# Splitting the operands of the second feed-forward half where they are made, and fetching them as two stored parts

## The chip, the core and the metric

The kernel runs on one core of one Trainium2 chip. The core has five engines that run side by side, each working through its own queue in order: TensorE (PE, with its weight loads as PEld), VectorE (DVE), ScalarE (ACT), GpSimd (POOL) and SyncE (SP), which here only issues transfers. Sixteen DMA engines move the data between HBM and the on-chip memory; a transfer can be issued from SP's, ScalarE's or GpSimd's queue. The metric is the device time of one execution in microseconds, lower being better.

## The reference

One inference step of a one-layer encoder on 640 frames (512 of a prompt, 8 x 16 of samples) of width 2048: an input projection, two groups of attention heads, an output projection, and a gated feed-forward layer of width 5632. The change touches only the feed-forward layer:

```python
def merge_and_ffn(x, oa, ob, norm_grp_a, norm_grp_b, w_out, norm_ffn, w_gate, w_up, w_down):
    o = jnp.concatenate([rmsnorm(oa, norm_grp_a), rmsnorm(ob, norm_grp_b)], axis=-1)
    x = x + o @ w_out
    h = rmsnorm(x, norm_ffn)
    return x + (jax.nn.silu(h @ w_gate) * (h @ w_up)) @ w_down
...
    y_prompt = rmsnorm(xp, norm_final)
    y_sample = rmsnorm(xs, norm_final)
```

## The kernel before

Everything is kept transposed, features on the 128 partitions and the 640 frames in two halves of `HT` = 320 columns along the row. All matrix products are of 32-bit values in TensorE's rounded format, and to keep the precision each operand is written as the sum of two rounded parts: `hi`, a rounded copy made by ScalarE, and `lo`, the rest, made by a subtraction on VectorE or GpSimd. `mm3` (lines 186 to 190) then issues three matmuls, hi x hi, hi x lo and lo x hi. Weights are split the same way after they are loaded: `split`, line 179 on ScalarE and line 180 on VectorE.

**Quartets.** The feed-forward products use a scheme with seven block products in place of eight (`quartet`, lines 870 to 922). Four weight blocks are loaded by SP (line 890); VectorE makes two differences of them (903 and 905), GpSimd two more (907 and 914); then come the products in the order p1, p6, p7, p2, p5, p4, p3. Each product splits its weights, multiplies them with `k` pairs of operands and leaves a PSUM bank that VectorE adds to the result tiles (line 924). The split weights lie in three pairs of tiles, so the split of a product waits until the product three before it has been read by TensorE. Of the weight tiles there are six, so loads run about one quartet ahead.

**The first half** (lines 957 to 1008). For each of the 22 pairs `i` of 128-row blocks of the inner width there is a quartet over `w_gate` and one over `w_up`, 44 in all, each of 7 x 8 x 3 matmuls. The left operands are the eight pairs of rows of the normed input, in seven combinations each, all held on the chip as split tiles (56 of the 62 tiles of list "S"). After the gate quartet VectorE, ScalarE and GpSimd apply the norm and the SiLU (990 to 992); after the up quartet VectorE multiplies gate and up (996), GpSimd makes four combinations (1000 to 1003: s1, s3, s2, s4), and the seven operands of the pair for the second half are stored unsplit to `act_d` in HBM, 128 x 320 values each, in four transfers (1005 and 1007), by SP, or by GpSimd for the last pair.

**The second half** (lines 1019 to 1064). The product with `w_down` runs in 32 steps. In a step five or six of the 22 pairs are active (`START`, `active`, lines 31 to 36); a pair stays for eight steps, one for each of eight pairs of output rows, which are kept in 20 tiles of "S". So the seven operands of a pair are fetched just before it becomes active. Pairs 0 to 4 are active at the start and come back at the end, so that 27 x 7 = 189 operands are loaded in all.

- `free` (946 to 955) is called after each product of the last quartet of the first half. It gives up the eight tiles of the combination just used and loads the operands of that combination for pairs 0 to 4, two pairs to a transfer, and splits them: `hi` on ScalarE (line 936), `lo` on VectorE for pairs 0, 2 and 4 and on GpSimd for 1 and 3 (line 941).
- `fetch` (928 to 944) does it for one operand. It loads the 160 KB into a spare "S" tile or one of two scratch tiles `half` (line 934), makes `hi` on ScalarE (936) and `lo` by a subtraction (941) on VectorE (combinations 0, 3 and 6) or GpSimd. In steps 16 to 29 it makes `lo` another way: ScalarE writes minus `hi` (938), and a GpSimd transfer loads the operand again and adds it (939).
- `fetch_waiting` keeps the fetches of a combination back until two more products have been issued.

The order of instructions in each engine's queue is made by a scheduler from the order of the program and the dependencies; a tile is written again only when all that read it, transfers included, are done.

## Time and profile before

| | |
|---|---|
| Median of three runs | 2653.87 us (2651.46 to 2653.96) |
| Profiled execution | 2658.85 us, of which the span from first to last instruction is 2657.1 us |
| PE busy | 2590.4 us, 97% |
| DVE, ACT, POOL busy | 1894.7, 1112.5 and 765.4 us |
| HBM read and written | 284.70 and 54.20 MB |
| Transfers on the hardware queue and on GpSimd's queue | 326.92 and 11.47 MB |
| Granted TensorE clock, mean | 0.992 |

The stages can be told apart by the lines that run in them: the first half of the feed-forward layer fills 1000 to about 2060 us, the 32 steps over `w_down` about 2060 to 2643 us, and the last 14 us scale and store the output.

How to read the rows: an engine's busy time counts its instructions, not its waits. A row of the view of groups gives line, engine, operation, output and inputs, the shape, the count, then busy time and mean nanoseconds of one, then the idle time of the engine just before these instructions and what ended it. In the views of order, the bracket at the end of a row is that idle time. "W" are weight tiles, "S" tiles of activations, "dn" and "at" PSUM banks, "half" the scratch tiles. A wait is put down to the event that came last.

### The profile page before, as it was taken

To read this page: it belongs to the slowest core of one execution; us is meant where nothing else is said; L and a number is where in the kernel's file an instruction comes from. 1 tells how busy PE (TensorE), PEld (TensorE's weight loads), DVE (VectorE), ACT (ScalarE), POOL (GpSimd) and SP (SyncE) were. 2 spreads that over 40 slices of the span, in tenths; PEclk is the share of its full clock that TensorE was granted. 3 is DMA by queue.
4 is the path that set the end of the run, shared out by engine and by line. 5 is a ranking of instruction groups with operands and counts; after the bars stand their busy time and mean duration, and the time that the engine had idled before them with its cause. 6 is when DMAs were issued, how large, how long until landed. Compare 5 with 4: busy or idle time off the path is not lost.

```text
span 2657.1 us, 44937 instructions
## 1 busy us (share of the span) xinstructions
PE 2590.4 (97%) x17565; PEld 2532.0 (95%) x17565; DVE 1894.7 (71%) x2934; ACT 1112.5 (42%) x1830; POOL 765.4 (29%) x584
## 2 busy tenths in 40 slices
PE   8999999999999999999999999999999899999996
PEld 8999998999899999999999999999999899999996
DVE  5665566655866877676676677667667988878797
ACT  5443344444633543333333333333334444455553
POOL 0000000000211223433433433343345533444463
PEclk9999999999999999999999999999999899999998
DMA  5322232433655433333333333333335744467665
GB/s 169 106 72 80 90 103 87 129 119 128 221 179 182 155 118 101 118 105 103 123 99 112 119 105 105 114 105 108 119 103 167 222 135 126 134 152 179 154 154 154
DMA packets 162549, 342.58 MB, mean 129 GB/s; under 512 B 19072, under 2 KB 77440, under 8 KB 162336
## 3 DMA queue, kind: packets, MB, share of 16 engines
q1 hardware_dynamic: 151824, 326.92, 38.9%
q0 software_dynamic: 9360, 11.47, 2.7%
q8 instruction: 138, 2.26, 0.4%
q10 hardware_dynamic: 1152, 1.31, 0.1%
q14 instruction: 75, 0.61, 0.1%
HBM read 284.70 MB, written 54.20 MB: 128 GB/s over the span
## 4 chain that ended last, share of the span: by engine, by line
PE 70%; DVE 6%; DMA 3%; issue 2%; ACT 2%; SPq 0%; POOL 0%; DVEq 0%; ACTq 0%; POOLq 0%
PE dn L188 14%; PE dn L190 14%; PE dn L189 14%; PE at L188 9%; PE at L189 9%; PE at L190 9%; DVE W L180 2%; PE at L303 1%; DMA S<-act_d 1%; DVE S L924 1%; DMA W<-w_down 1%; DVE S L180 1%; DMA S<-cka 1%; ACT W L179 1%; DVE S L941 0%
## 5 line engine op out<-in xcount | busy, mean ns | idle before, releaser
L188 PE MATMUL dn<-S,W 128*128 128x320 f32 x3694 | 1161.4, 314 | 11.8 <-DVE S L924 5.5
L190 PE MATMUL dn<-S,W 128*128 128x320 f32 x3694 | 1148.6, 311 | 14.5 <-DVE W L180 14.3
L189 PE MATMUL dn<-S,W 128*128 128x320 f32 x3694 | 1146.6, 310 | 2.0 <-DVE S L180 1.1
L179 ACT ACTIVATE W<-W 128x1024 fp32r<-128x1024 f32 (+2 forms) x632 | 608.2, 963 | 1024.6 <-PE dn L189 538.5
L180 DVE TENSOR_TENSOR W<-W,W 128x1024 fp32r<-128x1024 f32 (+2 forms) x632 | 761.1, 1204 | 157.8 <-ACT W L179 152.6
L188 PEld LDWEIGHTS dn<-S,W 128*128 128x128 f32 x3694 | 697.3, 189 | 24.5 <-issue 9.2
L190 PEld LDWEIGHTS dn<-S,W 128*128 128x128 f32 x3694 | 696.9, 189 | 20.5 <-DVE W L180 19.1
L189 PEld LDWEIGHTS dn<-S,W 128*128 128x128 f32 x3694 | 697.4, 189 | 4.6 <-DVE S L180 1.3
L190 PE MATMUL at<-S,W 128*128 128x320 f32 x1594 | 494.6, 310 | 4.2 <-DVE W L180 4.1
L188 PE MATMUL at<-S,W 128*128 128x320 f32 x1594 | 493.5, 310 | 0.0
L189 PE MATMUL at<-S,W 128*128 128x320 f32 x1594 | 493.3, 309 | 0.0
L907 POOL TENSOR_TENSOR W<-W,W 128x1024 f32<-128x1024 f32 (+2 forms) x76 | 163.4, 2150 | 583.1 <-DVE W L180 502.0
L190 PEld LDWEIGHTS at<-S,W 128*128 128x128 f32 x1594 | 299.8, 188 | 7.7 <-DVE W L180 7.4
L189 PEld LDWEIGHTS at<-S,W 128*128 128x128 f32 x1594 | 300.1, 188 | 0.0
L188 PEld LDWEIGHTS at<-S,W 128*128 128x128 f32 x1594 | 300.0, 188 | 0.0
L924 DVE TENSOR_TENSOR S<-S,dn 128x320 f32<-128x320 f32 x358 | 164.2, 481 | 100.6 <-PE dn L190 99.4
L903 DVE TENSOR_TENSOR W<-W,W 128x1024 f32<-128x1024 f32 (+2 forms) x76 | 135.6, 1784 | 102.9 <-DMA W<-w_up 50.7
L914 POOL TENSOR_TENSOR W<-W,W 128x1024 f32<-128x1024 f32 (+2 forms) x76 | 165.4, 2177 | 105.9 <-DVE W L180 102.8
L924 DVE TENSOR_TENSOR S<-S,at 128x320 f32<-128x320 f32 x262 | 123.3, 480 | 71.2 <-PE at L190 71.2
L262 POOL TENSOR_TENSOR S<-S,S 128x640 f32<-128x640 f32 x40 | 74.6, 1865 | 156.6 <-ACT S L261 153.4
L905 DVE TENSOR_TENSOR W<-W,W 128x1024 f32<-128x1024 f32 (+2 forms) x76 | 82.8, 1090 | 33.4 <-DMA W<-w_gate 25.8
L517 POOL MEMSET S<- 80x640 f32 x9 | 6.3, 695 | 330.0 <-DMA ob_d<-S 212.2
(153 smaller groups left out, 2269.2 us busy)
## 6 DMA issues: line engine op xcount, KB each, us to landing
W<-w_gate SPq DMA_DIRECT2D x88, 512.0 KB
W<-w_up SPq DMA_DIRECT2D x88, 512.0 KB
W<-w_in SPq DMA_DIRECT2D x66, 512.0 KB
W<-w_down SPq DMA_DIRECT2D x64, 384.0 KB
W<-w_down SPq DMA_DIRECT2D x68, 320.0 KB
act_d<-S SPq DMA_DIRECT2D x63, 320.0 KB
half<-act_d SPq DMA_DIRECT2D x81, 160.0 KB
S<-act_d SPq DMA_DIRECT2D x80, 160.0 KB
```

The lines of the kernel that those rows point to most:

```text
L179: self.nc.scalar.activation(hi, src, AF.Identity)
L180: self.nc.vector.tensor_tensor(lo, src, f(hi), ALU.subtract)
L188: mm(out, a[0], b[0], start=first, stop=False)
L189: mm(out, a[0], b[1], start=False, stop=False)
L190: mm(out, a[1], b[0], start=False, stop=last)
L262: (eng or nc.gpsimd).tensor_tensor(ssq, ssq, sq, ALU.add)
L303: nc.tensor.transpose(out, src, n.ident)
L903: nc.vector.tensor_tensor(b12[:, w], b12[:, w], b22[:, w], sub)
L905: nc.vector.tensor_tensor(s6[:, w], b11[:, w], b12[:, w], sub)
L907: nc.gpsimd.tensor_tensor(b11[:, w], b22[:, w], s6[:, w], sub)
L914: nc.gpsimd.tensor_tensor(b21[:, w], b21[:, w], s6[:, w], sub)
L924: add = lambda o, a, b: nc.vector.tensor_tensor(o, a, b, ALU.add)
```

## The change

The split moves from the second half into the first. When a pair is finished, its seven operands are put on a list `parts`; `store_part` takes one from the list at a time: ScalarE makes `hi` into a scratch tile, VectorE makes `lo` (over the operand itself, or for pairs 0 to 3 into another scratch tile), and SP stores both to `act_d`, which now has room for two parts. One part is handled at the end of the pair, one after each further product of the next gate quartet, and for the last pair one after each product of step 0. A result tile goes back to its list when its parts are stored, and the second result tile of each quartet is taken only after p6.

A fetch is then one transfer of 320 KB from GpSimd's queue into the tile, with no arithmetic. Only `free` still splits, for pairs 0 to 3, from unsplit copies that are stored beside (`first_d`); pair 4 is fetched.

```diff
-    def fetch(j, which, raw=None, engine=nc.gpsimd):
...
+    def fetch(j, which):
+        t = n.get("S")
+        hl = pack(t, HT)
+        nc.gpsimd.dma_start(out=r(sh(t, 2, HT)), in_=r(act_d[which, :, j]))
         lefts[j][which] = t, hl
 
     def free(which):
         n.put("S", *(h[which][0] for h in hs))
         ready = active(0)
-        for j in ready[::2]:
-            k = min(2, ready[-1] + 1 - j)
+        for j in ready[:-1:2]:
             raw = n.get("S")
-            dma(out=sh(raw, k, HT), in_=act_d[which, :, j:j + k])
-            for a in range(k):
-                fetch(j + a, which, raw[:, a * HT:a * HT + HT], (nc.vector, nc.gpsimd)[a])
+            dma(out=sh(raw, 2, HT), in_=first_d[which, :, j:j + 2])
+            for a, engine in enumerate((nc.vector, nc.gpsimd)):
+                t = n.get("S")
+                hi, lo = hl = pack(t, HT)
+                part = raw[:, a * HT:a * HT + HT]
+                nc.scalar.activation(hi, part, AF.Identity)
+                engine.tensor_tensor(lo, part, f(hi), ALU.subtract)
+                lefts[j + a][which] = t, hl
             n.put("S", raw)
+        fetch(ready[-1], which)
+
+    parts = []
+
+    def store_part():
+
+        if parts:
+            j, which, src, done = parts.pop(0)
+            if j < len(active(0)) - 1:
+                dma(out=first_d[which, :, j], in_=src)
+            hi = n.scratch()
+            nc.scalar.activation(r(hi), src, AF.Identity)
+            if j < len(active(0)) - 1:
+                lo = n.scratch()
+                nc.vector.tensor_tensor(r(lo), src, hi, ALU.subtract)
+            else:
+                lo = src
+                nc.vector.tensor_tensor(r(lo), src, hi, ALU.subtract)
+            dma(out=act_d[which, :, j, 0], in_=hi)
+            dma(out=act_d[which, :, j, 1], in_=lo)
+            n.put("S", *done)
...
-            y = n.get("S"), n.get("S")
-            c11, c21, c12, c22 = y[0][:, :HT], y[0][:, HT:], y[1][:, :HT], y[1][:, HT:]
+            y = [n.get("S")]
+            c11, c21 = y[0][:, :HT], y[0][:, HT:]
...
                 elif step == "p6":
+                    y.append(n.get("S"))
+                    c12, c22 = y[1][:, :HT], y[1][:, HT:]
                     add(c12, c11, bank)
...
+                if step != "p1":
+                    store_part()
...
-                store = nc.gpsimd.dma_start if i == NPAIR - 1 else dma
-                store(out=act_d[0, :, i], in_=c11)
-                for t, pick in ((w, slice(1, 7, 5)), (u, slice(2, 4)), (y[1], slice(4, 6))):
-                    store(out=act_d[pick, :, i].rearrange("w p c -> p w c"), in_=halves(t))
-                n.put("S", *gate, *y)
+                parts = [(i, 0, c11, [y[0]]), (i, 1, s2, []), (i, 6, s4, [w]), (i, 2, s3, []),
+                         (i, 3, s1, [u]), (i, 4, c12, []), (i, 5, c22, [y[1]])]
+                store_part()
```

24 lines of the change are left out of this document (5 added, 19 removed).

## The prediction

> **What bounds the kernel now.** I read the page's busy shares first, then stretches of 20 to 300 us, then the waits of each engine, and last the order of instructions at a pair boundary. First the page:
>
> ```profile
> span 2657.1 us, 44937 instructions
> ...
> PE 2590.4 (97%) x17565; PEld 2532.0 (95%) x17565; DVE 1894.7 (71%) x2934; ACT 1112.5 (42%) x1830; POOL 765.4 (29%) x584
> ```
>
> TensorE is the bound almost everywhere, so an edit pays only where PE loses time. The view of stretches shows where (columns: length, busy time and count of PE, PEld, DVE, ACT, POOL, granted clock, DMA share, GB/s). The first row is one gate quartet; the others belong to the turn from the first half into w_down and to the w_down stage:
>
> ```profile
> 1513.90:1538.50 24.60, 24.60 (x170) 24.60 (x169) 16.42 (x18) 8.50 (x9) 9.34 (x7) 1.00 0.43 140
> ...
> 2040.00:2060.00 20.00, 16.83 (x111) 15.88 (x109) 20.00 (x23) 15.38 (x34) 12.74 (x11) 1.00 0.79 262
> 2060.00:2080.00 20.00, 15.26 (x69) 14.26 (x70) 19.85 (x23) 7.12 (x15) 16.21 (x16) 0.66 0.72 242
> 2080.00:2100.00 20.00, 18.58 (x123) 17.69 (x122) 18.70 (x28) 9.12 (x17) 7.68 (x7) 1.00 0.75 234
> ...
> 2180.00:2200.00 20.00, 17.89 (x121) 17.39 (x120) 17.26 (x25) 9.74 (x17) 7.68 (x6) 1.00 0.46 133
> 2200.00:2500.00 300.00, 300.00 (x2047) 300.00 (x2046) 242.56 (x326) 146.45 (x235) 126.08 (x97) 1.00 0.60 150
> 2500.00:2600.00 100.00, 93.93 (x617) 90.17 (x616) 85.76 (x128) 56.15 (x102) 55.39 (x45) 1.00 0.65 152
> 2600.00:2620.00 20.00, 14.09 (x78) 12.33 (x77) 19.08 (x27) 9.65 (x19) 10.56 (x8) 0.91 0.46 141
> ```
>
> Undisturbed, a matmul takes 300/2047 = 0.1466 us. At that pitch the rows lose: 20 - 111 x 0.1466 = 3.7 us, then 9.9 and 2.0 (the turn, 15.6 together), 2.3 at 2180, 9.5 in 2500 to 2600, 8.6 in 2600 to 2620. The prize is 36 us; the gate quartet has nothing to win and something to lose. PE's waits after 2060 us, and behind them those of ACT and DVE in 2500 to 2600 and after 2600 (us, times, longest):
>
> ```profile
> PE dn L190 <- DVE W L180: 9.4, 9, 2.4
> PE dn L188 <- DVE S L924: 5.5, 3, 3.1
> PE at L190 <- DVE W L180: 4.1, 8, 1.6
> PE dn L188 <- ACT S L936: 2.9, 2, 2.1
> ```
> ```profile
> ACT S L936 <- DMA S<-act_d: 23.4, 11, 3.5
> ```
> ```profile
> DVE W L180 <- ACT W L179: 6.7, 5, 1.8
> DVE W L903 <- DMA W<-w_down: 5.6, 6, 1.6
> ```
> ```profile
> ACT S L936 <- DMA S<-act_d: 5.4, 5, 2.1
> ```
> ```profile
> DVE W L180 <- ACT W L179: 3.9, 3, 3.5
> ```
>
> PE waits for VectorE. VectorE in turn waits for ScalarE's weight split (L179), which stands in ScalarE's queue behind the operand split L936, and L936 waits for its transfer. That chain is what the change takes out.
>
> **What is removed, and what each costs.** The operand work of the second half, by shape:
>
> ```profile
> L939 POOL DMA_DIRECT2D S<-act_d x63 | 55.3, 886 | 85.1 <-ACT S L938 71.4 <-PE at L190 7.6 <-PE dn L190 2.7
> L936 ACT ACTIVATE S<-S 128x320 fp32r<-128x320 f32 x108 | 47.7, 464 | 56.7 <-DMA S<-act_d 55.8 <-DVE S L941 0.6
> ...
> L941 POOL TENSOR_TENSOR S<-S,S 128x320 fp32r<-128x320 f32 x41 | 45.0, 1105 | 45.8 <-ACT S L936 33.3 <-PE dn L190 6.9 <-PE dn L189 5.3
> ...
> L936 ACT ACTIVATE S<-half 128x320 fp32r<-128x320 f32 x81 | 37.3, 460 | 14.7 <-DMA half<-act_d 12.4 <-POOL S L941 1.3 <-DVE S L941 0.8
> ...
> L941 DVE TENSOR_TENSOR S<-S,S 128x320 fp32r<-128x320 f32 x41 | 35.0, 875 | 1.8 <-ACT S L936 1.8
> ...
> L941 POOL TENSOR_TENSOR S<-half,S 128x320 fp32r<-128x320 f32 x25 | 32.5, 1303 | 51.0 <-ACT S L936 50.9
> ...
> L938 ACT ACTIVATE S<-S 128x320 fp32r<-128x320 f32 x63 | 29.5, 470 | 1.7
> ...
> L941 DVE TENSOR_TENSOR S<-half,S 128x320 fp32r<-128x320 f32 x19 | 10.3, 544 | 0.1
> ```
>
> That is 189 operands: 35 split in `free`, 154 fetched later. After the change 28 are still split in `free` (four pairs, seven operands), 14 subtractions on VectorE and 14 on GpSimd; 161 come by one GpSimd transfer. ScalarE loses 161 x 0.46 + 29.5 = 104 us, VectorE 46 subtractions, GpSimd 52. GpSimd gains 98 transfers (161 for 63) at 0.886: 87 us, against 52 x 1.18 = 61 us and the last pair's four stores gone; it stays about where it is.
>
> The turn. In 2030 to 2060 and 2060 to 2080, L941 alone (DVE, POOL):
>
> ```profile
> 2030.00:2060.00 30.00, 14.31 (x15) 14.33 (x12) 1.00 0.69 222
> 2060.00:2080.00 20.00, 6.83 (x8) 6.14 (x6) 0.66 0.72 242
> ```
>
> VectorE is full from 2040 to 2080. `free` now gives it 14 subtractions instead of 21: 7 x 14.31/15 = 6.7 us less. The last pair's seven parts bring back seven at 0.48 to 0.95, so 3.4 to 6.7 us, later and spread over step 0. Net 3.3 at best of VectorE's. In 2060 to 2080 PE is idle 4.7 of the 9.9 us; the other 5.2 is the clock, granted at 0.66 after a 2.1 us wait for L936. I take 3.3 plus half of 5.2: 6 us; bounds -3 (the parts cost more than `free` saves) and 13.
>
> At 2180 the 2.3 us are waits behind L936 and its subtractions; none is left: 2 us. In 2500 to 2600 VectorE gets back up to the 6.7 us that it waits for L179, while 5.6 for weights stay; PE's steps with no fetch lose too, so I take two thirds, 4.5 of 9.5 us (0 to 8). In 2600 to 2620 likewise the 3.9 us: 4 of 8.6 (0 to 7). Sum of gains: 6 + 2 + 4.5 + 4 = 16.5 us.
>
> **What is added, and what covers it.** Each pair now costs seven ScalarE copies and seven VectorE subtractions, six of them in the next gate quartet: 7 x 0.46 = 3.2 us on 8.50 and 7 x 0.54 to 0.95 = 3.8 to 6.7 us on 16.42, of 24.60. Both fit, VectorE with 1.5 us to spare at worst. Stores go from 4 to 14 on SP's queue (21 for the first four pairs), 1.1 to 2.2 MB or about 46 GB/s more on 140, at a DMA share of 0.43. Where do they stand? At a pair's end today (VectorE, GpSimd, SP, PE):
>
> ```profile
> 1521.31 0.49 DVE L924 TENSOR_TENSOR S<-S,dn 128x320 f32<-128x320 f32 x1 [0.99 <-PE dn L190]
> 1524.46 1.23 DVE L903 TENSOR_TENSOR W<-W,W 128x1024 f32<-128x1024 f32 x1 [2.66 <-DMA W<-w_up]
> 1525.61 1.22 DVE L180 TENSOR_TENSOR W<-W,W 128x1024 fp32r<-128x1024 f32 x1
> ```
> ```profile
> 1517.40 0.88 POOL L1002 TENSOR_TENSOR S<-S,S 128x320 f32<-128x320 f32 x1
> ```
> ```profile
> 1515.48 4.14 SPq L1007 DMA_DIRECT2D act_d<-S  x3
> 1519.71 0.42 SPq L890 DMA_DIRECT2D W<-w_up  x1
> ```
> ```profile
> 1527.98 0.31 PE L188 MATMUL dn<-S,W 128*128 128x320 f32 x1
> 1528.13 0.31 PE L189 MATMUL dn<-S,W 128*128 128x320 f32 x1
> 1528.27 0.31 PE L190 MATMUL dn<-S,W 128*128 128x320 f32 x1
> ```
>
> Today SP sits in the stores, and a weight load behind them goes out only at 1519.71; VectorE waits 2.66 us for it, then does the split that ends at 1526.83 and is read at 1528.27: 1.4 us of slack, the smallest that I found in the first half. With stores spread over the quartet that load can go sooner (below nothing: a small gain, but PE is full, so worth 0); a store that waits for a late subtraction can block it as today. I price the first half at 0.
>
> The new fetch waits in GpSimd's own queue for a free tile, ahead of L907 and L914, for whose results the weight splits of p5 and p4 wait. In the L939 row GpSimd already waits 13 us for PE in 63 such transfers, and 2200 to 2500, which holds most of them, loses nothing. I take 1.5 us (0 to 8).
>
> The landing: GpSimd's issue and, on the same line, the time to landing:
>
> ```profile
> L939 POOL DMA_DIRECT2D S<-act_d x63: 842/857/1187, 2342.7 to 2591.9; - x63
> ...
> DMA to landing us min/median/max: 3.4/4.5/8.2
> ```
>
> A GpSimd load of 320 KB that only copies isn't in this trace; the nearest is this one, of 160 KB with an addition, and I take its median, with 3.4 and 8.2 as ends. A group is fetched two products after its tiles are freed and read five products later; a product of five operands is 15 x 0.1466 = 2.2 us, so 11 us of cover for 0.86 + 4.5 (9.1 with the longest).
>
> One rule speaks against the change. The row: 63 issues took 842 to 1187 ns while VectorE was 81 to 86% busy, so at most 0.35 us was lost to anything. The Trainium skill, "SBUF — State Buffer", section "Summary: rules for kernel authors", advises the hardware queues, since a VectorE instruction in a two-port mode keeps GpSimd from writing descriptors. By the row the sum stands; by the rule it turns over (the last rival). The same page, section "Who interferes with whom", excepts tensor_tensor, by inference; every VectorE line quoted here is one.
>
> Sum: 16.5 - 1.5 = 15 us off the profiled execution's 2658.85, so 2643.9. That execution is 4.98 above the median of 2653.87; from the median it is 2639.
>
> **The rivals.**
> 1. *VectorE stays the bound.* The turn only trades `free`'s seven subtractions for the last pair's seven, and the last steps are held by VectorE's own work (85.76 of 100) and its 5.6 us for weights. Left are 2 us at 2180 and 1 at the end: 2651. For it: VectorE at 20.00 of 20. Against: 10.6 us of VectorE's waits for L179.
> 2. *Slower: a landing enters VectorE's queue in the gate quartet.* The quartet's second result tile is now taken after p6, and it is the tile whose first half is being stored. From the fifth pair on that half is overwritten in place, so its subtraction waits for L1002 (until 1518.28), and its store must land before L924 may write. With 0.5 for the subtraction, 0.4 for the issue and the landings in the last fence, that is 1522.6 (3.4), 1523.7 (4.5) or 1527.4 (8.2), against 1521.31 today. L903 and L180 stand behind it (0.49 + 1.23 + 1.22), so it decides from a landing of 6.1 us; with 8.2 the split ends at 1530.3, 2.1 us late. At 1.3 us in each of the 17 pairs stored in place before the last it costs 22: 2639 + 22 = 2661. Against: L903 already starts as late as 1524.46, so ordinary landings find room.
> 3. *The operand itself becomes late.* If a fetch sits 2 us behind other GpSimd work, the longest landing misses the 11 us; about 0.7 us for each of the 17 pairs that enter after step 0: 12, and 2651.
> 4. *Descriptors are starved.* Each step one fetch is held for a VectorE operation, 0.875 us, ahead of L914; 30 steps: +26, 2665. Against: the 1187 ns above.
>
> **How the numbers follow.** Forecast 0.66, rivals 0.13, 0.12, 0.05, 0.04. A run of this kernel can tell 0.2%, 5.3 us, from no change. Faster 0.66; same 0.13 + 0.05 = 0.18; slower 0.12 + 0.04 = 0.16. The range runs from 2624 (30 us: 13, 2, 8 and 7 of the four places) to 2660, which takes in rivals 1 and 3 and the lighter half of 2.
>
> **What would show it.** Right: L936 and L941 left with 28 each; no ACT wait for act_d after 2100; the turn's 60 us with some 350 matmuls instead of 303 and the clock not below 0.8; 2500 to 2600 with about 648; the gate quartet still 24.6 us. Wrong: PE waits for L180 between 1100 and 2000, PE waits for a DMA from act_d, issues of the fetch over 1.2 us, or VectorE still at 20 of 20 up to 2100 with PE no fuller.

## The result, and the profile after

The changed kernel takes 2694.3 us (median of 4, 2692.9 to 2698.8) where the kernel before, on the same chip, takes 2653.9 (median of 4). The ratio is 1.0149, with a 95% interval of 1.0137 to 1.0161. It is slower by 40 us; the forecast was 2639. The profiled execution is 2693.0 us with a span of 2691.2, against 2657.1. The spans lie only 34 us apart, because the profiled execution of the kernel before is 5 us above its median and that of the changed kernel 1 us below.

The page of the changed kernel, its busy shares and two of its groups:

```profile
span 2691.2 us, 45286 instructions
...
PE 2597.8 (97%) x17565; PEld 2536.1 (94%) x17565; DVE 1983.5 (74%) x3042; ACT 1078.0 (40%) x1760; POOL 754.6 (28%) x626
...
L960 ACT ACTIVATE half<-S 128x320 fp32r<-128x320 f32 x154 | 72.4, 470 | 262.8 <-DMA act_d<-half 117.5
...
L932 POOL DMA_DIRECT2D S<-act_d x161 | 87.9, 547 | 190.7 <-PE dn L190 96.3
```

The matmuls are the same 17565 and every engine's share moved by at most three points, so no engine became full. What stands out is one group: the new copies L960 themselves cost 72 us, but ScalarE idles 263 us ahead of them, 117.5 of these until a store from a scratch tile has landed.

**Where the time went.** Four marks that both kernels have divide the second part of the run: the first and the last ScalarE copy of a p1 bank in the first half, and the same copy in steps 0 and 7 of the second half. The order of instructions on ScalarE, before:

```profile
968.53 0.42 ACT L967 ACTIVATE S<-dn 128x320 f32<-128x320 f32 x1
...
2037.14 0.42 ACT L967 ACTIVATE S<-dn 128x320 f32<-128x320 f32 x1
...
2065.55 0.44 ACT L1043 ACTIVATE S<-dn 128x320 f32<-128x320 f32 x1 [1.40 <-PE dn L190]
...
2186.45 0.42 ACT L1043 ACTIVATE S<-dn 128x320 f32<-128x320 f32 x1
```

and after (the columns are start, length, engine, line):

```profile
965.38 0.42 ACT L981 ACTIVATE S<-dn 128x320 f32<-128x320 f32 x1
...
2076.69 0.42 ACT L981 ACTIVATE S<-dn 128x320 f32<-128x320 f32 x1
...
2109.59 0.42 ACT L1058 ACTIVATE S<-dn 128x320 f32<-128x320 f32 x1
...
2228.93 0.42 ACT L1058 ACTIVATE S<-dn 128x320 f32<-128x320 f32 x1
```

The differences give a ledger: first half 1068.6 us before and 1111.3 after (+42.7), turn 28.4 and 32.9 (+4.5), steps 0 to 7 120.9 and 119.3 (-1.6), from step 7 to the end of the span 470.7 and 462.3 (-8.4). With the 3.1 us by which the first mark lies earlier that is the 34.1 us between the spans. The same ledger is used for every kernel below; it comes from one profiled execution each, and three kernels with the same first half (e3, e5 and e8) lie within 4.2 us there, so a difference under some 4 us says nothing by itself.

The marks have a weakness: they are ScalarE's copies, and where ScalarE's queue is ordered anew a mark moves against the matmuls. Between the marks of the turn PE issues 145 matmuls before and 135 after, between those of steps 0 to 7 it issues 757 and 740. Counted by PE's own matmuls in order (the 6440th, 13690th, 13870th, 14600th and 16400th of the same 17565, then the end), the differences are +42.9 for the first half, +2.9 for the turn, +4.1 for steps 0 to 7, -1.5 up to about 2450 us and -9.3 for the rest. The first half stays as it is; turn and steps 0 to 7 together lose 7.0 us and not 2.9.

The view of stretches shows the same in matmuls. Before (a long piece of the first half, the turn, and the 120 us in which pairs 0 to 4 return):

```profile
1250.00:2040.00 790.00, 790.00 (x5389) 790.00 (x5388) 546.10 (x579) 273.60 (x293) 298.05 (x163) 1.00 0.34 111
...
2036.00:2066.00 30.00, 25.54 (x153) 23.81 (x151) 29.94 (x33) 19.89 (x46) 21.03 (x17) 0.90 0.81 264
...
2500.00:2620.00 120.00, 108.02 (x693) 102.51 (x692) 104.84 (x155) 65.80 (x120) 65.96 (x52) 0.99 0.62 150
```

After:

```profile
1250.00:2040.00 790.00, 773.93 (x5239) 769.99 (x5240) 623.70 (x673) 304.45 (x388) 306.90 (x155) 1.00 0.40 129
...
2077.00:2110.00 33.00, 22.18 (x135) 21.43 (x135) 32.58 (x31) 16.21 (x34) 27.34 (x31) 0.92 0.97 318
...
2535.00:2655.00 120.00, 113.35 (x749) 111.07 (x748) 102.83 (x155) 48.24 (x71) 60.13 (x57) 0.99 0.57 160
```

The first half had lost nothing and now lacks 150 of 5389 matmuls, 22 us at 0.1466; the return of the pairs gains 56 matmuls, 8.2 us; the turn is no fuller (135 matmuls in 33 us, 153 in 30 before).

What ScalarE waits for in the first half, 1000 to 2040 us, before and after (total, times, longest):

```profile
ACT W L179 <- PE at L189: 302.0, 124, 2.5
ACT W L179 <- PE dn L189: 287.5, 146, 2.5
```
```profile
ACT W L179 <- PE at L189: 179.2, 74, 4.1
ACT half L960 <- DMA act_d<-half: 102.4, 46, 5.1
...
ACT half L960 <- POOL S L1020: 71.1, 20, 4.9
```

Before, its waits were mostly for PE, that is for tiles of split weights that PE had still to read, so ScalarE stood ready ahead of its weight splits. Now it stands 102 us behind stores that must land and 71 us behind one of GpSimd's combinations, with weight splits queued behind it. How that reaches PE is seen at one pair boundary. The order of instructions in the changed kernel, VectorE, GpSimd, SyncE and PE:

```profile
1541.08 0.49 DVE L966 TENSOR_TENSOR S<-S,half 128x320 fp32r<-128x320 f32 x1 [1.73 <-POOL S L1020]
1542.35 1.00 DVE L966 TENSOR_TENSOR S<-S,half 128x320 fp32r<-128x320 f32 x2 [0.77 <-POOL S L1021]
1543.80 1.23 DVE L180 TENSOR_TENSOR W<-W,W 128x1024 fp32r<-128x1024 f32 x1 [0.45 <-ACT W L179]
...
1552.95 1.23 DVE L906 TENSOR_TENSOR W<-W,W 128x1024 f32<-128x1024 f32 x1 [2.63 <-DMA W<-w_up]
...
1554.49 1.22 DVE L180 TENSOR_TENSOR W<-W,W 128x1024 fp32r<-128x1024 f32 x1
```
```profile
1545.10 3.33 POOL L915 TENSOR_TENSOR W<-W,W 128x1024 f32<-128x1024 f32 x1 [2.79 <-DVE W L180]
```
```profile
1548.46 0.33 SPq L891 DMA_DIRECT2D W<-w_up  x1
1548.89 0.38 SPq L967 DMA_DIRECT2D act_d<-half  x1
```
```profile
1555.77 0.41 PE L190 MATMUL at<-S,W 128*128 128x320 f32 x1 [1.04 <-DVE W L180]
```

and ScalarE at the same place:

```profile
1553.41 0.47 ACT L960 ACTIVATE half<-S 128x320 fp32r<-128x320 f32 x1 [3.88 <-DMA act_d<-half]
1554.23 0.47 ACT L960 ACTIVATE half<-S 128x320 fp32r<-128x320 f32 x1 [0.35 <-DVE W L906]
1554.61 1.99 ACT L179 ACTIVATE W<-W 128x1024 fp32r<-128x1024 f32 x2
```

Read it as one chain. The in-place subtractions L966 hold VectorE 1.73 and 0.77 us until GpSimd has read the tiles; the weight split behind them starts at 1543.80; GpSimd's weight difference L915 waits for that split and ends at 1548.43; only then is a weight tile free, and SyncE's load goes out at 1548.46; VectorE waits 2.63 us for it, the next split ends at 1555.71, and PE loses 1.04 us. The high half's store stands behind the same load (1548.89), and the copy that needs its scratch tile waits, on ScalarE, until 1553.41, ahead of two weight splits.

### The profile page after: what moved, and what is told of

It reads as the page before. It is cut to its first block, busy times and chain, and to the rows that moved or that the text cites. A ratio compares the mean times of both kernels' runs of the same rounds, so it can differ in the third digit from the quotient of the medians.

```text
span 2691.2 us, 45286 instructions
## 1 busy us (share of the span) xinstructions
PE 2597.8 (97%) x17565; PEld 2536.1 (94%) x17565; DVE 1983.5 (74%) x3042; ACT 1078.0 (40%) x1760; POOL 754.6 (28%) x626
## 4 chain that ended last, share of the span: by engine, by line
PE 55%; DVE 12%; DMA 9%; POOL 4%; issue 3%; ACT 2%; SPq 0%; DVEq 0%; ACTq 0%; POOLq 0%
PE dn L188 11%; PE dn L190 11%; PE dn L189 11%; PE at L190 7%; PE at L188 7%; PE at L189 6%; DMA W<-w_up 5%; DVE W L180 4%; POOL W L915 2%; DVE S L925 2%; DMA act_d<-half 2%; DVE W L906 1%; PE at L303 1%; DMA W<-w_down 1%; DVE S L1014 1%
## 5 line engine op out<-in xcount | busy, mean ns | idle before, releaser
L179 ACT ACTIVATE W<-W 128x1024 fp32r<-128x1024 f32 (+2 forms) x632 | 605.2, 961 | 830.3 <-PE dn L189 409.8
L180 DVE TENSOR_TENSOR W<-W,W 128x1024 fp32r<-128x1024 f32 (+2 forms) x632 | 744.3, 1178 | 95.7 <-ACT W L179 93.4
L190 PEld LDWEIGHTS at<-S,W 128*128 128x128 f32 x1594 | 300.8, 189 | 34.8 <-DVE W L180 34.7
L908 POOL TENSOR_TENSOR W<-W,W 128x1024 f32<-128x1024 f32 (+2 forms) x76 | 163.6, 2153 | 588.0 <-DVE W L180 367.6
L915 POOL TENSOR_TENSOR W<-W,W 128x1024 f32<-128x1024 f32 (+2 forms) x76 | 177.8, 2339 | 141.5 <-DVE W L180 135.1
L960 ACT ACTIVATE half<-S 128x320 fp32r<-128x320 f32 x154 | 72.4, 470 | 262.8 <-DMA act_d<-half 117.5
L904 DVE TENSOR_TENSOR W<-W,W 128x1024 f32<-128x1024 f32 (+2 forms) x76 | 124.5, 1638 | 69.6 <-DMA W<-w_down 34.7
L925 DVE TENSOR_TENSOR S<-S,at 128x320 f32<-128x320 f32 x262 | 123.3, 480 | 40.9 <-PE at L190 40.4
L906 DVE TENSOR_TENSOR W<-W,W 128x1024 f32<-128x1024 f32 (+2 forms) x76 | 82.9, 1090 | 80.8 <-DMA W<-w_up 49.4
L932 POOL DMA_DIRECT2D S<-act_d x161 | 87.9, 547 | 190.7 <-PE dn L190 96.3
```

The costliest lines, as they stand in the source:

```text
L179: self.nc.scalar.activation(hi, src, AF.Identity)
L180: self.nc.vector.tensor_tensor(lo, src, f(hi), ALU.subtract)
L190: mm(out, a[1], b[0], start=False, stop=last)
L904: nc.vector.tensor_tensor(b12[:, w], b12[:, w], b22[:, w], sub)
L906: nc.vector.tensor_tensor(s6[:, w], b11[:, w], b12[:, w], sub)
L908: nc.gpsimd.tensor_tensor(b11[:, w], b22[:, w], s6[:, w], sub)
```

## The experiments

The theories are A (the landing of the stores that read the scratch tiles: A1 their place in SyncE's queue, A2 the landing itself), B (VectorE's load), C (the doubled stores in SyncE's queue), D (copies and subtractions that wait for GpSimd's combinations ahead of weight splits); for the turn S (VectorE and GpSimd slow each other) and T (transfers). In the tables, "first five" are the first ten quartet intervals.

| kernel | time, us (runs) | first half (first five + rest) | turn | steps 0-7 | to the end |
|---|---|---|---|---|---|
| before | 2653.9 (4) | 1068.6 (254.2 + 814.4) | 28.4 | 120.9 | 470.7 |
| after | 2694.3 (4) | 1111.3 (273.2 + 838.1) | 32.9 | 119.3 | 462.3 |
| e1_no_split | 2656.8 (1) | 1072.2 (255.2 + 817.0) | 28.9 | 125.8 | 463.3 |
| e2_scratch_unread | 2666.3 (1) | 1083.8 (259.8 + 824.0) | 33.1 | 118.3 | 462.0 |
| e3_act_store | 2681.0 (1) | 1096.9 (270.3 + 826.6) | 33.5 | 118.3 | 462.8 |
| e4_whole | 2698.7 (4) | 1104.0 (257.0 + 847.0) | 45.5 | 119.2 | 461.5 |
| e5_step_later | 2684.6 (2) | 1098.5 (269.5 + 829.0) | 33.5 | 119.0 | 462.5 |
| e6_pool_sub | 2700.4 (2) | 1116.6 (266.9 + 849.6) | 33.4 | 119.0 | 461.9 |
| e7_first_deferred | 2672.9 (3) | 1086.6 (255.6 + 831.0) | 30.1 | 128.5 | 464.9 |
| e8_turn_vector | 2675.0 (2) | 1094.3 (266.4 + 828.0) | 27.6 | 121.0 | 463.2 |
| e9_other_data | 2717.7 (2) | 1135.1 (305.5 + 829.7) | 32.9 | 120.4 | 460.2 |
| e10_no_sub | 2661.4 (8) | 1075.7 (257.5 + 818.2) | 33.0 | 119.8 | 462.3 |
| e11_return_only | 2650.4 (10) | 1068.4 (254.4 + 814.0) | 35.1 | 116.6 | 461.9 |
| e12_both | 2669.5 (2) | 1084.4 (256.5 + 827.9) | 31.8 | 123.3 | 462.1 |
| e13_pair_data | 2658.3 (8) | 1073.2 (255.0 + 818.2) | 34.8 | 118.8 | 461.8 |
| e14_return_vector | 2648.8 (10) | 1068.8 (254.7 + 814.1) | 31.8 | 120.7 | 460.7 |
| e15_return_four | 2656.0 (10) | 1068.8 (254.9 + 813.9) | 35.1 | 118.6 | 465.4 |

The kernel before ran at 2654.2 to 2654.9 beside all of these.

**e1_no_split**, on the changed kernel: stores and fetches as they are, no arithmetic on the parts.

```diff
-            hi = n.scratch()
-            nc.scalar.activation(r(hi), src, AF.Identity)
...
-            dma(out=act_d[which, :, j, 0], in_=hi)
-            dma(out=act_d[which, :, j, 1], in_=lo)
+            dma(out=act_d[which, :, j, 0], in_=src)
+            dma(out=act_d[which, :, j, 1], in_=src)
```

> Leaves out the split of the parts: each operand is stored twice as it is, so ScalarE and VectorE do nothing for it and no scratch tile is used; the values fetched are wrong. The stores and their place in SyncE's queue stay. Measure: the first half, from the first to the last copy of p1's result, 1068.6 us before and 1111.3 after the change. Theory A (landing: ScalarE's copy of a part waits for a scratch tile until an earlier store has landed, with the weight split behind it): 1069 to 1073. Theory B (load: 154 more subtractions are too much for VectorE): the same, 1069 to 1073. Theory C (SyncE: the doubled stores keep the weight loads back): 1090 or more. Theory D (ScalarE's copy waits in its queue for GpSimd's combinations): 1069 to 1073. The rest, from there to the end, 620.0 before and 614.5 after: 605 to 612 by A, since step 0 loses its scratch waits too.

The first half falls to 1072.2, only 3.6 us above the kernel before. So the doubled stores and their place in SyncE's queue are not the cause by themselves (C falls as the main one); 39 of the 42.7 us come from the copies and subtractions and what they wait for. The run is also, in effect, the change's second half alone. From the last mark of the first half to the end it takes 618.0 us, the changed kernel 614.5, the kernel before 620.0: even a free first half would have brought 2 to 6 us, not 15.

**e2_scratch_unread**, on the changed kernel: the arithmetic kept, both stores read the operand's own tile.

```diff
-            dma(out=act_d[which, :, j, 0], in_=hi)
-            dma(out=act_d[which, :, j, 1], in_=lo)
+            dma(out=act_d[which, :, j, 0], in_=src)
+            dma(out=act_d[which, :, j, 1], in_=src)
```

> Keeps ScalarE's copy into a scratch tile and VectorE's subtraction, but both transfers read the operand's own place, so that no transfer reads a scratch tile and its next writer never waits for a landing; both stored parts are the low part, so the values are wrong. Theory A (landing): first half falls from 1111.3 to 1080 or less. Theory B (load on VectorE): stays at 1105 to 1111. Theory C (SyncE's queue): stays above 1100. Theory D (GpSimd's combinations ahead of the weight split): 1090 to 1100, the first four pairs better and the others still 1.3 us each.

27.5 of the 42.7 us go when no transfer reads a scratch tile: theory A has the largest part. 11.6 us above e1 remain, so not all of it; 1083.8 lies between what was expected of A alone and of D alone.

**e3_act_store**, on the changed kernel: only the high half's store moves, from SyncE's queue to ScalarE's.

```diff
-            dma(out=act_d[which, :, j, 0], in_=hi)
+            nc.scalar.dma_start(out=act_d[which, :, j, 0], in_=hi)
```

> The transfer of the high part is issued from ScalarE's own queue right behind the copy, not from SyncE's, where it can stand behind a weight load that waits for its tile. If the scratch tile is late because of its place in SyncE's queue (theory A1), the first half falls from 1111.3 to 1090 or less. If the landing itself is what lasts (A2), it stays at 1105 or more. ScalarE pays about 0.8 us an issue (its eight output transfers took 6.29 us), 5.5 us a pair, which it has. B and D: no change.

The first half falls by 14.4, about half of what e2 took out, and the run by 13. That lies between the two expectations, so each of A1 and A2 has a part, and A1 is that half. (An issue took ScalarE 0.33 us in the median, not the 0.8 expected.) ScalarE's waits in 1000 to 2040 us now read:

```profile
ACT half L960 <- POOL S L1020: 73.0, 21, 4.3
ACT half L960 <- DMA act_d<-half: 39.7, 32, 4.2
```

102.4 us of landing became 39.7; the wait for GpSimd is what it was. The other half lies mostly in the first five pairs (270.3 against 259.8 in e2), the first four of which use both scratch tiles for every part.

**e4_whole**, on the changed kernel: parts made from whole tiles into one wide scratch tile in place of two narrow ones, and the first four pairs not split in their quartets but stored at the turn from the tiles split there.

```diff
+    def part_tile(i, t, pick):
+        s = n.scratch()
+        nc.scalar.activation(r(s), t, AF.Identity)
+        nc.vector.tensor_tensor(r(t), t, s, ALU.subtract)
+        for k, x in enumerate((s, t)):
+            dma(out=act_d[pick, :, i, k].rearrange("w p c -> p w c"), in_=halves(x))
```

> Splits whole tiles: the two scratch tiles become one of double width; the first operand is split into its two halves and stored by one transfer, the other six as three tiles of two, in place, after p7, p5 and p3, so four copies and subtractions a pair for seven and about 7 us between two uses of the scratch tile. Pairs 0 to 3 are stored unsplit as before the change, and their parts are stored from the tiles that the last quartet has split. Theory A (landing): first half 1069 to 1076, rest 610 to 618, total 2645 to 2656. Theory B (load): 1090 to 1096, since VectorE's work a pair hardly falls. Theory D: 1085 to 1095, since the copies still wait for GpSimd's combinations. Theory C: 1080 to 1090, with 7 stores for 14.

The first five pairs fall by 16, but the later ones get slower (847.0 against 838.1) and the turn grows to 45.5: the ratio is 1.0167 [1.0150, 1.0184]. The first half, 1104.0, is above what was expected of any theory. ScalarE's waits in 1250 to 2040 us show why the later pairs did not follow:

```profile
ACT whole L969 <- DMA act_d<-whole: 83.0, 30, 4.4
...
ACT whole L969 <- POOL S L1028: 72.0, 15, 5.8
```

One tile in place of two waits for every landing, and a wide part waits for two combinations. The edit changed two things at once; e7 repeats the second, the first four pairs, alone.

**e5_step_later**, on e3: the parts one product later.

```diff
-                if step != "p1":
-                    store_part()
+                store_part()
```

> Edit, on the kernel that stores the high halves from ScalarE's queue (2681.0 us, span 2679.3): the parts of a pair are handled at all seven products of the next quartet, none right at the pair's end, so that each stands one product later in the queues of ScalarE and VectorE. There, between 1250 and 2040 us, ScalarE waits 52.8 us and VectorE 40 us for GpSimd's four combinations, 5.8 us a pair, and what stands behind them are the weight splits. Theory D (parts queued ahead of weight splits while they wait for GpSimd): these waits go, the quartet in which the parts are handled falls from 26.6 to about 25, the rest of the first half from 826.6 to 810-817, the run to about 2667. Theory B (VectorE is simply full in that quartet: its subtractions are added to sums and products that run at 2.2 to 3.4 us where GpSimd works beside them): the waits go and the quartet stays within 0.5 us, the run at 2675-2683. A third: the tile that the first part holds comes free one product later and the next quartet's second sum then waits for its store to land; VectorE's sums would show waits for DMA and the run is over 2685.

No test: the scheduler put the instructions in the same places, with the same waits (52.8 us for L1019, e3's L1020), and the run is e3's within 4 us. It serves as a repeat, and shows that moving a line in the program need not move an instruction in its queue.

**e6_pool_sub**, on e3: the parts' subtractions on GpSimd.

```diff
-                nc.vector.tensor_tensor(r(lo), src, hi, ALU.subtract)
+                nc.gpsimd.tensor_tensor(r(lo), src, hi, ALU.subtract)
```

> Edit, on the kernel that stores the high halves from ScalarE's queue: the subtraction of each part runs on GpSimd in place of VectorE. Theory B (VectorE's load): VectorE loses 7 x 0.48 us of work and 2.4 us of waits a pair, the quartet of the parts falls from 26.6 to 24.7-25.2, the rest of the first half from 826.6 to 814-818, the first five pairs from 270 to about 262, the run to 2655-2665. Theory D with ScalarE's copies as the cause: ScalarE still waits for the combinations, so the rest stays at 823-828 and the run at 2675-2683. A third, that VectorE and GpSimd slow each other whenever both run operations on two inputs: GpSimd works 7 x 0.9 to 1.8 us more a pair, VectorE's sums and products take longer than now (its product with the gate already 2240 ns where the kernel before shows 1233) and the run stays above 2681.

Slower by 19 us. GpSimd's groups in 1250 to 2040:

```profile
L966 POOL TENSOR_TENSOR S<-S,half 128x320 fp32r<-128x320 f32 x105 | 109.7, 1068 | 9.2 <-ACT half L960 9.2
L915 POOL TENSOR_TENSOR W<-W,W 128x1024 f32<-128x1024 f32 x31 | 89.5, 2886 | 20.1 <-DVE W L180 20.1
```

and its PE waits:

```profile
PE at L190 <- DVE W L180: 26.3, 15, 3.2
```

A subtraction costs 1068 ns there, and it stands ahead of L915, the link of the chain above; PE's waits for L180 in that stretch were 6.4 us in e3. ScalarE's copies L960 also wait 30.5 us there for these subtractions to read the scratch tile, and VectorE's weight splits wait 87.7 us for ScalarE's, 17.3 in e3. VectorE lighter by 7 subtractions a pair brought nothing, which speaks against B already.

**e7_first_deferred**, on e3: the first four pairs are stored whole and their parts are stored in steps 0, 1, 2 and 4, from the tiles of the turn.

```diff
+            k = {0: 0, 1: 1, 2: 2, 4: 3}.get(t)
+            if k is not None:
+                dma(out=act_d[which, :, k], in_=sh(lefts[k][which][0], 2, HT))
```

> Edit, on the kernel that stores the high halves from ScalarE's queue: the first four pairs are stored whole and nothing else is done with them in the first half; their two parts are stored in steps 0, 1, 2 and 4 of the second half, from the tiles that the turn has split anyway. Theory A/B (what the first four pairs cost is the splitting done in their quartets, with two scratch tiles a part): the first five pairs fall from 270.3 to 255-258, nothing else moves, the run at about 2667. Theory T (the 28 stores of 320 KB, 9.2 MB, come on top of transfers that already fill the turn): the turn and steps 0 to 7 grow from 33.5 and 118.3 by 9 to 13 us together, as the turn did in the kernel with whole tiles (45.5 against 32.9), and the run is at 2676-2681.

(The ledger is that of its longest run, 2679.0.) A/B has its range: the first five pairs fall by 14.7. T is seen in part: steps 0 to 7 give 10.2 back, with 3.4 gained in the turn, so 6.8 together and not 9 to 13. Steps 0 to 7, e3 and e7:

```profile
2098.00:2216.00 118.00, 112.49 (x736) 111.14 (x735) 87.41 (x135) 40.62 (x63) 44.47 (x54) 0.97 0.77 234
```
```profile
2084.00:2212.00 128.00, 114.85 (x734) 112.78 (x733) 90.36 (x135) 40.50 (x62) 48.22 (x59) 0.93 0.88 290
```

The same 735 matmuls take 10 us longer while 290 in place of 234 GB/s move. That the transfers are the cause is the likely reading; tiles held until their stores have landed would look alike here, and no run parts the two.

**e8_turn_vector**, on e3: the turn's 28 subtractions all on VectorE, none on GpSimd.

```diff
-            for a, engine in enumerate((nc.vector, nc.gpsimd)):
+            for a, engine in enumerate((nc.vector, nc.vector)):
```

> Edit, on the kernel that stores the high halves from ScalarE's queue: the 28 subtractions at the turn all run on VectorE, none on GpSimd. In the turn of the changed kernel 13 of them took VectorE 1305 ns each and GpSimd's 13 took 1120 ns, against 484 ns for the same shape where VectorE works alone: both engines were busy all the time. Theory S (the two slow each other, and the turn's price is that): 28 x 0.48 to 0.6 us is 13 to 17 us, no more than the 16.6 us that VectorE now spends on 13 of them, and the turn shortens from 33.5 to 29-31, the run by 2 to 4 us. Theory T (the turn is full of transfers: share 0.97, 318 GB/s in the changed kernel against 0.81 and 264 before): the turn stays at 33-34 though VectorE is lighter. Theory L (VectorE's number of operations sets it): 28 x 1.3 us, the turn grows by over 10 us.

S holds here: the turn falls from 33.5 to 27.6 us; turn and steps 0 to 7 together fall by 3.2, which is within the 4 us. The subtractions of the turn by engine, in the changed kernel (VectorE, then GpSimd):

```profile
L946 DVE TENSOR_TENSOR S<-S,S 128x320 fp32r<-128x320 f32 x13 | 16.5, 1305 | 0.0
```
```profile
L946 POOL TENSOR_TENSOR S<-S,S 128x320 fp32r<-128x320 f32 x13 | 14.4, 1120 | 0.1
```

and in e8, with its stretch:

```profile
L946 DVE TENSOR_TENSOR S<-S,S 128x320 fp32r<-128x320 f32 x26 | 13.8, 581 | 1.1 <-ACT S L945 1.0
```
```profile
2060.00:2087.00 27.00, 22.21 (x135) 21.02 (x133) 25.89 (x42) 15.53 (x32) 13.84 (x20) 0.94 1.09 381
```

Twice the subtractions in less time, with more transferred beside them, 381 GB/s against 318; so it was not the transfers that made one cost 1305 ns. Whether the transfers are the next bound of the turn was not tested.

**e9_other_data**, on e2: the arithmetic on the norm's factors, which are ready early (the result lacks the split).

```diff
+            own = src if j == NPAIR - 1 else r_f[:, :HT]
+            nc.scalar.activation(r(hi), own, AF.Identity)
+            nc.vector.tensor_tensor(r(lo), own, hi, ALU.subtract)
```

> Edit, on the kernel whose scratch tiles no transfer reads (span 2664.2): the copy and the subtraction of each part are made on the tile of the norm's factors, which has long been ready, and both into scratch; the parts themselves are stored unsplit, twice. The arithmetic is thus left out of the result, but its instructions stand in the queues as before, and wait for nothing that GpSimd makes. Between 1250 and 2040 us the kernel with the unread scratch still waits 52 us on ScalarE and 40 us on VectorE for GpSimd's combinations. Theory D (the waits cost): the quartet of the parts falls from 26.5 to about 25, the first half from 1083.8 to 1073-1076 (without any arithmetic it was 1072.2, before 1068.6), the run to about 2656. Theory B (the work itself costs, 7 copies and 7 subtractions a pair): the first half stays at 1080-1084, the run at 2662-2666.

A miss: with nothing to wait for, the scheduler placed nearly all of it in the quartets of the first pairs. The groups of 1000 to 1370 us hold 147 of the 154 subtractions:

```profile
L962 DVE TENSOR_TENSOR half<-S,half 128x320 fp32r<-128x320 f32 x147 | 124.0, 844 | 31.5 <-ACT half L961 30.3
...
L961 ACT ACTIVATE half<-S 128x320 fp32r<-128x320 f32 x146 | 68.1, 466 | 184.6 <-DVE half L962 184.6
```

The pairs after them ran at 24.6 to 24.7 us a quartet, but without any load. It decides nothing between B and D; e13 does.

**e10_no_sub**, on e2: no subtraction, ScalarE's copy kept.

```diff
-                nc.vector.tensor_tensor(r(lo), src, hi, ALU.subtract)
```

> Edit, on the kernel whose scratch tiles no transfer reads: the subtraction of each part is left out, ScalarE's copy into the scratch tile stays; both stores read the unsplit part. Theory B with VectorE as the full engine: the first half falls from 1083.8 to 1072-1075, to what it is without any arithmetic, the run to about 2656. Theory D with ScalarE's copies as the ones in the way (52 us of waits for GpSimd between 1250 and 2040): the first half stays above 1079. Between the two, each takes its share.

8.1 of the 11.6 us go, though ScalarE still waits 52.7 us for the combinations in 1250 to 2040. What remains of D sits in VectorE's queue, not in ScalarE's; B is still possible.

**e13_pair_data**, on e2: copy and subtraction on the pair's c12 in place of the parts, into the scratch tile; the same number, nearly the same places, but nothing of GpSimd's to wait for.

```diff
-            nc.scalar.activation(r(hi), src, AF.Identity)
+            nc.scalar.activation(r(hi), own[0], AF.Identity)
+            nc.vector.tensor_tensor(r(hi), own[0], hi, ALU.subtract)
...
+                own[0] = c12
```

> Edit, on the kernel whose scratch tiles no transfer reads (span 2664.2, rest of the first half 824.0): each copy and subtraction of a pair is made on that pair's c12, ready when VectorE has multiplied gate and up, and into the scratch tile; the parts are stored unsplit, twice, so the split is left out of the result. The number of instructions and nearly their places in the queues stay (VectorE: all seven subtractions still between the product with the gate and the next sums of weights), but none waits for GpSimd's combinations. Theory D (waiting in the queue ahead of weight splits): the rest of the first half falls from 824.0 to 815-818, the run to about 2656-2659. Theory B (VectorE's number of operations): the rest stays at 822-826 and the run at 2662-2668.

The first half is 1073.2, within 1.0 us of the kernel without any arithmetic. PE's waits in 1000 to 2030, e2 and then e13:

```profile
PE dn L190 <- DVE W L180: 8.9, 20, 1.2
```
```profile
PE at L190 <- DVE W L180: 2.8, 6, 0.9
PE dn L190 <- DVE W L180: 0.3, 1, 0.3
```

D holds and B falls. The edit also frees the stores from waiting for the subtractions, but that isn't the gain: between 1250 and 2040 us the stores wait longer in SyncE's queue here than in e2, 144.5 us against 97.7. So 154 copies and 154 subtractions cost nothing that can be measured as long as they don't wait for GpSimd or a landing, although VectorE is busier than in e2 (669.6 of these 790 us, 636.1 in e2).

**e11_return_only**, on the kernel before: its first half and its fetches, but the operands of pairs 0 to 4, split at the turn anyway, are stored as parts in steps 0 to 6, and their return is one GpSimd transfer each.

```diff
+                if j in active(0):
+                    back = n.get("S")
+                    lefts[j][which] = back, pack(back, HT)
+                    nc.gpsimd.dma_start(out=r(sh(back, 2, HT)), in_=r(split_d[which, :, j]))
+                    continue
...
+            k = {0: 0, 1: 1, 3: 2, 4: 3, 6: 4}.get(t)
+            if k is not None:
+                dma(out=split_d[which, :, k], in_=sh(lefts[k][which][0], 2, HT))
```

> Edit, on the kernel before: its first half and its turn as they are, every fetch as it is but one kind. The operands of pairs 0 to 4, split at the turn anyway, are stored as two parts from their tiles in steps 0, 1, 3, 4 and 6 (35 transfers of 320 KB, nothing computed), and their second visit (steps 24 to 31) fetches them with one transfer each from GpSimd's queue. Theory R (what the change gained in the second half, 8.4 us from step 7 to the end, lies where pairs 0 to 4 return, 2500 to 2620 us, and needs no splitting in the first half): first half and turn as before, steps 0 to 7 at 120.9 plus 0 to 3 for the stores, the rest 470.7 down to 462-464, the run 4 to 9 us under the kernel before. Theory T (stores of 11.5 MB in steps 0 to 6 collide as in the kernel that deferred four pairs, +10 us there): steps 0 to 7 take 128-131 and the run is within 3 us of the kernel before, or slower.

2650.4 against 2654.5 us: a ratio of 0.9986 [0.9976, 0.9996], faster than both kernels, by little. The first half is as before and the end 461.9, 8.8 us shorter; the 120 us of the return hold

```profile
2490.00:2610.00 120.00, 113.50 (x750) 110.94 (x749) 103.93 (x154) 48.85 (x71) 59.61 (x57) 0.99 0.56 160
```

as many matmuls as the changed kernel. Theory R holds: what the change gains late needs no splitting in the first half. By the marks the turn is 6.7 us longer and steps 0 to 7 are 4.3 shorter, but that is the mark, not PE. From mark to mark, before and in e11:

```profile
2037.14:2065.55 28.41, 24.40 (x145) 22.67 (x143) 28.41 (x33) 18.32 (x42) 19.46 (x15) 0.90 0.82 269
```
```profile
2034.20:2069.30 35.10, 29.11 (x166) 27.80 (x165) 32.02 (x39) 19.31 (x43) 24.36 (x23) 0.85 0.85 294
```

ScalarE copies the p1 bank of step 0 some 20 matmuls later. From PE's 13690th to its 13870th matmul e11 takes 37.5 us, the kernel before 39.2; the steps to the 14600th take 115.2 and 111.6. What the stores cost is thus some 3.6 us in steps 0 to 7, and nothing in the turn.

**e12_both**, on e3: the edits of e7 and e8 together.

> Edit, on the kernel that stores the high halves from ScalarE's queue: both repairs at once, the first four pairs' parts stored in steps 0, 1, 2 and 4 from the tiles of the turn, and the turn's 28 subtractions all on VectorE. If they add up: first five pairs 255.6, rest of the first half 826-831, turn 25-28, steps 0 to 7 128, rest 463: 2664 to 2669. If the stores in the first steps take back what the shorter turn gave (transfers at 381 GB/s there already): 2671-2675, no better than either alone. In neither case under the kernel before, since the later pairs' quartets (26.6) stay.

2669.5 (ratio 1.0055 [1.0033, 1.0076]), the best form of the change itself and between the two expectations. The turn gave 31.8, not 27.6: the deferred stores took back part of it.

**e14_return_vector**, on e11: the turn's subtractions all on VectorE (the same edit as e8's).

> Edit, on the kernel that stores split operands only for the return of pairs 0 to 4 (2650.4, turn 35.1, steps 0 to 7 116.6): the turn's 35 subtractions all on VectorE. Theory S (VectorE and GpSimd slow each other): 35 x 0.58 us is 20 us in place of 19 x 0.97 to 1.3 us, GpSimd is free for its weight differences; turn and steps 0 to 7 fall from 151.7 to 146-149, the run to 2645-2648. If VectorE's number of operations decides in this turn: 20 us and more on VectorE, 151-156, the run at 2650-2655.

2648.8, ratio 0.9981 [0.9972, 0.9991]. It can't be told from e11: by the marks the turn falls by 3.3 and steps 0 to 7 grow by 4.1, together 152.5, so the 146 to 149 of theory S did not come. The price did fall: in the turn a subtraction took VectorE 551 ns (33 of them) where e11 shows 927 (21, beside 13 on GpSimd). But by PE's count the turn takes 37.8 us for e11's 37.5, so here that price was not what held PE.

**e15_return_four**, on e11: pair 0 left out, stored and fetched as before.

```diff
-            k = {0: 0, 1: 1, 3: 2, 4: 3, 6: 4}.get(t)
+            k = {1: 1, 3: 2, 4: 3, 6: 4}.get(t)
```

> Edit, on the same kernel (2650.4): pair 0, whose stores fall into the turn and step 0, is left out, so that it is stored and fetched as in the kernel before; pairs 1 to 4 keep their stores in steps 1, 3, 4 and 6. Theory T (the seven stores of 320 KB, 2.3 MB, lengthen the turn): turn and steps 0 to 7 fall from 151.7 to 148-150 (149.3 before), the rest grows from 461.9 to 463-464 for the one pair that is split again; the run at 2648-2651. If the stores are not what lengthens the turn: 151-152 stays and the run is at 2651-2653.

2656.0, ratio 1.0007 [0.9998, 1.0017]. The turn stays at 35.1 (37.7 by PE's count, e11 37.5), so its seven stores cost it nothing that can be seen. Together with steps 0 to 7 it is 153.7, above both ranges. The one pair shows 3.5 us at the end, more than I had given it but within the 4 us; the run is 5.6 us slower than e11.

## Why the prediction was wrong

**The step that failed: "I price the first half at 0."** It measured 42.7 us. Its two supports were busy time ("VectorE with 1.5 us to spare at worst") and one slack (1.4 us). The first was right: e13 puts as many instructions there for 1.0 us over e1, which is not to be told from nothing. What it left out is that an instruction in an in-order queue costs its wait as well, and passes it to all that stand behind. By kernels the 42.7 divide into 3.6 for the stores alone (e1), 1.0 for the arithmetic (e13 over e1), 10.6 for waiting on GpSimd's combinations (e2 over e13) and 27.5 for scratch tiles that come free only when a store has landed (after over e2), of which 14.4 is the store's place in SyncE's queue (e3). The text saw SyncE's queue and asked only who else it delays; it didn't ask when the two scratch tiles come free, nor what VectorE's queue does while L1020 runs. These are sums over kernels whose queues the scheduler ordered anew each time, so the division holds to some 4 us a term: the two large ones stand, the two small ones are not resolved. Of the 10.6 us, 4.8 lie in the first five pairs, where e13 also needs one scratch tile for a part in place of two; 5.8 are the later pairs', where both use one.

**Rival 2** had the right family, a landing that blocks a queue in the quartet of the parts, and the wrong place: it priced the second result tile. The landing that counted was that of the scratch tiles. Its other remark, that the in-place subtraction waits for L1002 (L1020 after), was right, and is the chain shown above; I used it for one store only and not for the weight split behind it.

**The turn**, 6 us at 2040 to 2100 and 2 at 2180: the turn and steps 0 to 7 took 2.9 us more by the marks, 7.0 by PE's count. VectorE did get fewer subtractions, 13 for 19 in the two stretches, but each took 1305 ns where the kernel before shows 968:

```profile
L941 DVE TENSOR_TENSOR S<-S,S 128x320 fp32r<-128x320 f32 x19 | 17.8, 968 | 0.0
```

So VectorE was as full as before (32.58 of 33). The term assumed a fixed price for an operation whose price depends on GpSimd beside it. e8 shows that this was the cause of a good part: 581 ns and a turn of 27.6; in e14, on another kernel, the price fell too (927 to 551 ns), but by PE's count the turn did not get shorter. The transfers, at a share of 0.97 to 1.09, which the text didn't consider, may be a second bound; that isn't shown. This is rival 1 for the turn, but with another reason.

**The last steps**, 4.5 + 4 us: 8.4 measured by the marks, 9.3 by PE's count after some 2450 us. That the sum fits to a tenth is luck; its size is right. The chain (L936 waiting for its transfer ahead of L179) was read rightly, and e11 gets the same gain by taking it out for pairs 0 to 4 alone.

**The fetch**, 1.5 us: no wait of PE leads to it, and an issue took 547 ns, not the 886 of the accumulating one. The rival of starved descriptors did not come. The Trainium skill, "SBUF — State Buffer", section "Summary: rules for kernel authors", says that descriptor generation for GpSimd's transfers is starved while VectorE is in a 2x or 4x mode; by that rule the issues would have grown if VectorE's operations here were of that kind. The trace shows no growth: 161 issues, 87.9 us in all, beside a VectorE busy 102.83 of 120 us in the stretch above.

Of the signs named in advance, those of the fetch came as hoped: issues of 0.53 to 0.72 us, and no wait of PE for `act_d`. Those listed under wrong came too: PE waits for L180 between 1000 and 2040 us (22.1 us in 20 waits), and a VectorE that is full through the turn, whose 60 us (2080 to 2140) hold 253 matmuls where some 350 were forecast.

## What to carry to other kernels

Work moved into a stage that has busy time to spare is free only if its operands are ready when its turn comes in each in-order queue: ask for every inserted instruction what it waits for and what stands behind it, scratch tiles read by a store included, since those come free only at the landing. An operation's price is read from a stretch with the same neighbours, for two-input operations on VectorE and GpSimd above all. And before a whole transformation is moved, look where its gain lies: here five of 22 pairs held it, and for those the split tiles existed already.

## What the runs showed of the hardware

- An operation with two tiles as inputs takes VectorE longer while GpSimd runs such operations. The same 128x320 subtraction takes VectorE 581 ns on average in the turn of e8, where GpSimd runs none of them, and 1305 ns in the changed kernel, where they share the work; 551 ns in e14 and 927 in e11. Putting all of them on VectorE made the turn shorter in e8; in e14, by PE's count, it did not. The Trainium skill, "SBUF — State Buffer", section "Who interferes with whom", says that a VectorE instruction with two inputs in SBUF (the on-chip memory that holds the tiles) contends with a GpSimd instruction that reads SBUF; the trace agrees.
- A GpSimd transfer that copies 320 KB is issued in 547 ns (mean of 161, changed kernel); the 160 KB one with an addition took 886 (mean of 63, kernel before).
- A stored scratch tile came free late even when its store was small: in the boundary shown, a copy waits until 1553.41 us for a 160 KB store issued at 1548.89, 4.5 us, and before its issue that store had stood in SyncE's queue since the tile was written at 1544.93, 4.0 us.
